# Spreading the 32x32 inversions of an RWKV-7 mixer over all 128 partitions of GpSimd

## The chip, the cores and the metric

The kernel runs on one core of one Trainium2 chip. The core has a matmul engine (TensorE, in the profile PE), a vector engine (DVE), a scalar engine (ACT), a general engine (GpSimd, in the profile POOL) and a queue that mostly issues transfers (SP). ACT and POOL issue transfers too. The metric is the device time of one execution in microseconds (us), from three runs.

## The reference, cut to what matters

The program computes two layers of a streaming encoder over 512 frames of width 1024. Layer 0 has two mixers side by side, HGRN2 (four heads of 128) and RWKV-7 (eight heads of 64), then a feed-forward block. Layer 1 has an S5 and an mLSTM mixer, then another feed-forward block. The change touches the RWKV-7 mixer alone. Its recurrence per head is

```python
def step(state, inp):
    r_t, w_t, k_t, v_t, a_t, b_t = inp
    sa = jnp.einsum("bhvk,bhk->bhv", state, a_t)
    state = (state * w_t[:, :, None, :] + sa[..., None] * b_t[:, :, None, :]
             + v_t[..., None] * k_t[:, :, None, :])
    return state, jnp.einsum("bhvk,bhk->bhv", state, r_t)
```

The kernel does this in chunks of 64 frames. Within a chunk the term with `sa` makes a triangular system: one strictly triangular 64x64 matrix per head and chunk, of which the inverse of one plus it (up to sign) is wanted. The kernel inverts the two 32x32 blocks on the diagonal of each and joins them by matmuls afterwards.

## The kernel before, in words

Activations lie as features x frames, so a matmul of the dense projections has 128 features of weights standing and 512 frames moving. Weights are f32; each is split into a rounded part `hi` (ACT, L375) and a rest `lo` (DVE or, for a few units, POOL, L376), and three matmuls into the PSUM tile `d` stand for one exact product. Those `d` matmuls are most of PE's work.

While PE does the dense projections of layer 0 (generator `dense`, called F), the mixers run beside it. `PRM["prog"]` lists seven stages; in each, `weave` takes turns between F up to a marker and one or two RWKV-7 generators, by the numbers that they yield. For RWKV-7 the eight heads make four pairs p, two pairs a group q, and the eight chunks make two halves g, so each kind of work comes four times, once for each (q, g):

- `rwp` (gates and `rw_prep`): elementwise work on DVE and ACT and small matmuls into PSUM tiles `r`. At its end four ACT-issued transfers per pair write the 32x32 blocks of `pb` to the scratch tensor `scr_a` in HBM.
- `inv` (`rw_inverse`): reads the 32 blocks of (q, g) into the tile `iu`, one block per partition, sets the diagonal to one, and sweeps: step j of 1 to 30 multiplies column j above the diagonal by row j to its right (`ti`, L987) and adds it to the rows above (L989). Both are POOL instructions. The result goes to `scr_u` in HBM (L991).
- `rwd` (`rw_solve` and `rw_chain`): eight transfers (L1000) bring the blocks of `scr_u` into the block-diagonal tile `ub`, then matmuls `r<-y,ub` and so on solve the system and carry the state from chunk to chunk.

The stages are: F alone; rwp(0,0); inv(0,0) with rwp(0,1); inv(0,1) with rwd(0,0); rwd(0,1) with rwp(1,0); inv(1,0) with rwp(1,1); inv(1,1) with rwd(1,0). F stands beside all but the last. After them rwd(1,1) runs beside the first part of layer 0's output projection (`outa`, matmuls `d<-ysp`).

The HGRN2 head in F has a chain of its own: for each of six levels an elementwise difference of `c` (`e<-c`, partly on POOL, partly on DVE), an exponential on ACT, two products on DVE (`e<-e,u` and `e<-e,k`) and matmuls `m<-e`.

The order in which the code emits instructions is not final. A scheduler of the framework places them by its own model of their durations, engine by engine, under the data dependencies; every engine then executes its list strictly in order. All tiles of the pool `pl` are allocated once, and `iu` and `ti` have one buffer each. Transfers of the inversions (`dq(1)`, `dq(2)`, `dq(3)`) are all issued by POOL, those into `scr_a` by ACT.

Of the kernel before, what the change touches and what calls it, by code (L numbers as in the profile page):

```python
# [10 lines left out]
F32 = mybir.dt.float32  # L11
# [4 lines left out]
ADD, SUB, MUL, MAX, MIN = ALU.add, ALU.subtract, ALU.mult, ALU.max, ALU.min  # L16

P = 128
# [184 lines left out]
def trunk(ctx: ExitStack, tc: tile.TileContext, A, out, dbg=None, start=0):  # L203
    nc = tc.nc
    V, S, G, T = nc.vector, nc.scalar, nc.gpsimd, nc.tensor
# [103 lines left out]
    if start < 1:  # L309
        for s in PRM["seq"]:  # L310
            nm, a, b = {"L": ("wB", 0, 1), "P": ("wB", 1, 3), "H": ("wA", 0, 4)}[s[0]]
# [54 lines left out]
    def wget(nm):  # L366
        assert order[pos[0]][0] == nm, (nm, order[pos[0]])
        while pos[1] <= pos[0] + AHEAD and pos[1] < len(order):
            wissue()
        pos[0] += 1  # L370
        return ready[pos[0] - 1]
# [283 lines left out]
    def layer0():  # L655
# [43 lines left out]
        scr_a = dram.tile([2, 2, 2, 2, 2, 4, 32, 32], F32, name="scr_a")  # L699
        scr_u = dram.tile([2, 2, 2, 2, 2, 4, 32, 32], F32, name="scr_u")  # L700
# [4 lines left out]
        N2 = 256  # L705
# [4 lines left out]
        pl = sl.pool("rw")  # L710
# [181 lines left out]
        def dq(j):  # L892
            return {"s": nc.sync, "g": G, "a": S}[PRM["dq"][j]]
# [84 lines left out]

        def rw_inverse(q, g):

            iu = pl.tile([32, 32, 32], F32, tag="iu", name="iu")
            dq(1).dma_start(iu, scr_a[q, g].rearrange("p h b c s t -> (p h b c) s t"))
            G.memset(iu.rearrange("p a b -> p (a b)")[:, 0:1024:33], 1.0)
            for j in range(1, 31):
                n = 31 - j
                t3 = pl.tile([32, N2], F32, tag="ti", name="ti")[:, 0:j * n].rearrange("p (a b) -> p a b", b=n)
                G.tensor_tensor(t3, iu[:, j:j + 1, j + 1:].to_broadcast([32, j, n]),  # L987
                                iu[:, 0:j, j:j + 1].to_broadcast([32, j, n]), MUL)
                G.tensor_tensor(iu[:, 0:j, j + 1:], iu[:, 0:j, j + 1:], t3, ADD)  # L989
                yield 1.2  # L990
            dq(2).dma_start(scr_u[q, g].rearrange("p h b c s t -> (p h b c) s t"), iu)  # L991

        def rw_solve(g, p):
            R = which[g, p]
# [136 lines left out]
        sa = Pools()  # L1131
        pa = sa.pool("hg", side="right")
        kinds = dict(rwp=rwp, rwd=rwd, inv=rw_inverse, gates=rw_gates, prep=rw_prep, solve=rw_solve, chain=rw_chain)

        def build(s):
# [87 lines left out]
    if start < 1:  # L1223
# [5 lines left out]
        for u in range(4):  # L1229
            w = wget("wO0b")  # L1230
            for i in range(2):
                n = 2 * u + i
# [445 lines left out]
    for u in range(4):  # L1678
        w = wget("wO1b")
        for i in range(2):  # L1680
            n = 2 * u + i
# [67 lines left out]
```

## Time and profile before

| what | value |
|---|---|
| time, median of 3 runs | 1464.06 us (1461.65 to 1466.17) |
| the profiled execution's own time | 1462.31 us |
| its span, first to last instruction | 1460.5 us |
| PE busy | 1400.2 us, 96% |
| DVE busy | 961.2 us, 66% |
| ACT busy | 681.1 us, 47% |
| POOL busy | 354.0 us, 24% |
| mean granted clock of PE | 0.976 |

The span is 1.8 us shorter than the profiled execution's time. A group row of the profile reads: line, engine, operation, out<-in by tile names, shapes, count, then busy us and mean ns of one, then the idle time of the engine just before such instructions and what ended it. A window row gives, for a stretch of the span, each engine's busy us, the clock that PE was granted (1.00 is full) and the share of the 16 DMA engines in use. The four inversions lie at about 91 to 134, 156 to 194, 273 to 314 and 333 to 375 us.

### The profile page before, as it was taken

To read this page: it belongs to the slowest core of one execution; us is meant where nothing else is said; L and a number is where in the kernel's file an instruction comes from. 1 tells how busy PE (TensorE), PEld (TensorE's weight loads), DVE (VectorE), ACT (ScalarE), POOL (GpSimd) and SP (SyncE) were. 2 spreads that over 40 slices of the span, in tenths; PEclk is the share of its full clock that TensorE was granted. 3 is DMA by queue.
4 is the path that set the end of the run, shared out by engine and by line. 5 is a ranking of instruction groups with operands and counts; after the bars stand their busy time and mean duration, and the time that the engine had idled before them with its cause. 6 is when DMAs were issued, how large, how long until landed. Compare 5 with 4: busy or idle time off the path is not lost.

```text
span 1460.5 us, 19910 instructions
## 1 busy us (share of the span) xinstructions
PE 1400.2 (96%) x6668; PEld 1136.9 (78%) x6668; DVE 961.2 (66%) x2041; ACT 681.1 (47%) x1594; POOL 354.0 (24%) x538
## 2 busy tenths in 40 slices
PE   8989999988999999999999899999999999999996
PEld 5877878766787788888888678766678888888885
DVE  7588679899688656555444688678776555554433
ACT  7554565636365333344333333477554434433332
POOL 5367650668420333110010542100020000000001
PEclk9988999999999999999999999999999999999998
DMA  5311221111323332333343842410133233333331
GB/s 180 94 38 46 64 72 52 30 46 58 118 84 97 101 116 91 113 108 106 105 125 105 206 113 80 116 58 28 56 105 90 99 101 96 92 102 94 93 114 61
DMA packets 51142, 133.39 MB, mean 91 GB/s; under 512 B 10640, under 2 KB 16272, under 8 KB 50784
## 3 DMA queue, kind: packets, MB, share of 16 engines
q1 hardware_dynamic: 38656, 116.86, 26.4%
q0 software_dynamic: 3024, 7.26, 2.1%
q10 hardware_dynamic: 9360, 8.00, 1.8%
q8 instruction: 53, 0.87, 0.2%
q14 instruction: 49, 0.40, 0.1%
HBM read 121.71 MB, written 10.39 MB: 90 GB/s over the span
## 4 chain that ended last, share of the span: by engine, by line
PE 76%; DVE 11%; POOL 4%; ACT 4%; DMA 2%; issue 2%; ACTq 0%; SPq 0%; DVEq 0%; POOLq 0%
PE d L292 63%; PE m L292 7%; PE r L292 5%; DVE lo L376 2%; POOL iu L989 1%; POOL ti L987 1%; DVE e L277 1%; DMA raw<-in_wV_dram 1%; ACT s L253 1%; DVE hl L467 1%; DVE ks L277 1%; ACT hi L375 0%; DVE u L277 0%; POOL ks L277 0%; DMA x<-in_xT_dram 0%
## 5 line engine op out<-in xcount | busy, mean ns | idle before, releaser
L375 ACT CAST hi<-raw 128x256 fp32r<-128x256 f32 (+1 forms) x809 | 317.4, 402 | 502.1 <-PE d L292 446.8
L376 DVE TENSOR_TENSOR lo<-raw,hi 128x256 fp32r<-128x256 f32 (+1 forms) x774 | 348.3, 460 | 280.5 <-ACT hi L375 269.6
L292 PE MATMUL d<-hh,hi 128*128 128x512 f32 x1088 | 436.1, 401 | 3.6 <-DVE ur L1086 2.4
L292 PE MATMUL d<-hh,lo 128*128 128x512 f32 x1088 | 431.4, 397 | 0.0
L292 PE MATMUL d<-hl,hi 128*128 128x512 f32 x1088 | 430.2, 395 | 0.0
L292 PEld LDWEIGHTS d<-hh,hi 128*128 128x128 f32 x1088 | 207.1, 190 | 48.0 <-DVE ur L1086 3.0
L292 PEld LDWEIGHTS d<-hh,lo 128*128 128x128 f32 x1088 | 206.8, 190 | 43.7 <-issue 1.5
L292 PEld LDWEIGHTS d<-hl,hi 128*128 128x128 f32 x1088 | 206.9, 190 | 43.3 <-issue 2.3
L292 PE MATMUL d<-ah,hi 128*128 128x512 f32 x330 | 128.4, 389 | 0.0
L292 PE MATMUL d<-al,hi 128*128 128x512 f32 x330 | 128.4, 389 | 0.0
L292 PE MATMUL d<-ah,lo 128*128 128x512 f32 x330 | 128.4, 389 | 0.0
L1718 POOL TENSOR_TENSOR x<-x,f 128x256 f32<-128x256 f32 x6 | 5.2, 889 | 358.8 <-issue 352.3
L292 PE MATMUL d<-ysp,hi 128*128 128x512 f32 x224 | 75.3, 411 | 2.7 <-DVE x L1685 1.5
L473 POOL TENSOR_TENSOR rstd<-rstd,sq 128x512 f32<-128x512 f32 x21 | 28.8, 1373 | 196.8 <-ACT sq L253 196.7
L989 POOL TENSOR_TENSOR iu<-iu,ti 32x30 f32<-32x30 f32 (+14 forms) x120 | 70.8, 590 | 9.2
L292 PEld LDWEIGHTS d<-ah,hi 128*128 128x128 f32 x330 | 61.9, 188 | 13.0
L292 PEld LDWEIGHTS d<-ah,lo 128*128 128x128 f32 x330 | 61.9, 188 | 12.8
L292 PEld LDWEIGHTS d<-al,hi 128*128 128x128 f32 x330 | 61.9, 188 | 12.8
L987 POOL TENSOR_TENSOR ti<-iu 32x30 f32<-32x30 f32 (+14 forms) x120 | 68.9, 574 | 9.0
L292 PEld LDWEIGHTS d<-ysp,hi 128*128 128x128 f32 x224 | 42.2, 193 | 12.9 <-DVE x L1685 2.3
L292 PE MATMUL d<-ysp,lo 128*128 128x512 f32 x112 | 45.5, 406 | 0.0
L1197 DVE TENSOR_TENSOR g<-d,g 128x512 f32<-128x512 f32 x42 | 29.0, 691 | 24.1 <-PE d L292 24.1
(490 smaller groups left out, 2043.0 us busy)
## 6 DMA issues: line engine op xcount, KB each, us to landing
raw<-in_wGU_dram SPq DMA_DIRECT2D x88, 512.0 KB, 3.6
raw<-in_wD_dram SPq DMA_DIRECT2D x32, 512.0 KB, 3.5
raw<-in_wA_dram SPq DMA_DIRECT2D x16, 512.0 KB, 3.7
raw<-in_wB_dram SPq DMA_DIRECT2D x13, 512.0 KB, 3.7
raw<-in_wD_dram SPq DMA_DIRECT2D x16, 384.0 KB, 3.1
raw<-in_wV_dram SPq DMA_DIRECT2D x6, 512.0 KB, 5.7
raw<-in_wQ_dram SPq DMA_DIRECT2D x6, 512.0 KB, 3.6
raw<-in_wK_dram SPq DMA_DIRECT2D x6, 512.0 KB, 3.7
```

Of the source, the lines that this page charges most:

```text
L253: a = S.activation(o, i, f, bias=bias, scale=scale)
L277: on(op, i, j).tensor_tensor(o, a, b, f)
L292: T.matmul(o, w, a, start=start, stop=stop)
L375: S.copy(h, src)
L376: eng.tensor_tensor(l, src, h.bitcast(F32), SUB)
L467: V.scalar_tensor_tensor(self.hl[:, k, :], x, pc(self.g, k), self.hh[:, k, :].bitcast(F32), MUL, SUB)
L473: self.eng.tensor_tensor(self.rstd, self.rstd, sq, ADD)
L987: G.tensor_tensor(t3, iu[:, j:j + 1, j + 1:].to_broadcast([32, j, n]), iu[:, 0:j, j:j + 1].to_broadcast([32, j, n]), MUL)
L989: G.tensor_tensor(iu[:, 0:j, j + 1:], iu[:, 0:j, j + 1:], t3, ADD)
L1197: V.tensor_tensor(g1, pu_, g1, MUL)
L1718: G.tensor_tensor(x[k][:, t], x[k][:, t], r_, MUL)
```

## The change

The 32 blocks of one (q, g) are laid on 128 partitions: partition 32k + n holds, of block n, the rows k, k+4, k+8 and so on, eight rows in the tile `iw`. Row j, which every partition needs at step j and which no earlier step alters, is read from a full copy of the block in `iu`, so each of the four groups of 32 partitions has its own copy. Step j then covers ceil(j/4) rows on every partition instead of j rows on a quarter of them; rows at or below j are zero in column j and stay as they are. The diagonal of ones is set at the end, in four pieces. The loads become eight transfers (four of 32 KB, four of 128 KB), the store four (32 KB each), all still issued by POOL. The generator yields 0.6 a step instead of 1.2.

```diff
         def rw_inverse(q, g):
-            iu = pl.tile([32, 32, 32], F32, tag="iu", name="iu")
-            dq(1).dma_start(iu, scr_a[q, g].rearrange("p h b c s t -> (p h b c) s t"))
-            G.memset(iu.rearrange("p a b -> p (a b)")[:, 0:1024:33], 1.0)
+            iu = pl.tile([P, 32, 32], F32, tag="iu", name="iu")
+            iw = pl.tile([P, 8, 32], F32, tag="iw", name="iw")
+            blocks = scr_a[q, g].rearrange("p h b c s t -> (p h b c) s t")
+            for k in range(4):
+                w = slice(32 * k, 32 * k + 32)
+                dq(1).dma_start(iw[w], blocks.rearrange("n (r k) t -> n k r t", k=4)[:, k])
+                dq(1).dma_start(iu[w], blocks)
             for j in range(1, 31):
-                n = 31 - j
-                t3 = pl.tile([32, N2], F32, tag="ti", name="ti")[:, 0:j * n].rearrange("p (a b) -> p a b", b=n)
-                G.tensor_tensor(t3, iu[:, j:j + 1, j + 1:].to_broadcast([32, j, n]),
-                                iu[:, 0:j, j:j + 1].to_broadcast([32, j, n]), MUL)
-                G.tensor_tensor(iu[:, 0:j, j + 1:], iu[:, 0:j, j + 1:], t3, ADD)
-                yield 1.2
-            dq(2).dma_start(scr_u[q, g].rearrange("p h b c s t -> (p h b c) s t"), iu)
+                n, m = 31 - j, (j + 3) // 4
+                t3 = pl.tile([P, 80], F32, tag="ti", name="ti")[:, 0:m * n].rearrange("p (a b) -> p a b", b=n)
+                G.tensor_tensor(t3, iu[:, j:j + 1, j + 1:].to_broadcast([P, m, n]),
+                                iw[:, 0:m, j:j + 1].to_broadcast([P, m, n]), MUL)
+                G.tensor_tensor(iw[:, 0:m, j + 1:], iw[:, 0:m, j + 1:], t3, ADD)
+                yield 0.6
+            for k in range(4):
+                w = slice(32 * k, 32 * k + 32)
+                G.memset(iw[w].rearrange("p a b -> p (a b)")[:, k:256:36], 1.0)
+                dq(2).dma_start(scr_u[q, g].rearrange("p h b c s t -> (p h b c) s t")
+                                .rearrange("n (r k) t -> n k r t", k=4)[:, k], iw[w])
```

What the scheduler makes of it differs in three places that matter below. The first is POOL's list at the start of the first inversion, before the change (`e` and `c` are tiles of the HGRN2 head, `lo`, `raw` and `hi` the split of a weight):

```order
L982 DMA iu<-scr_a 32x1024
L376 TENSOR_TENSOR lo<-raw,hi 128x256
L983 MEMSET iu 32x32
L987 TENSOR_TENSOR ti<-iu 32x30
L989 TENSOR_TENSOR iu<-iu,ti 32x30
L987 TENSOR_TENSOR ti<-iu 32x58
L277 TENSOR_TENSOR e<-c 128x8x32
L277 TENSOR_TENSOR e<-c 128x16x16
L989 TENSOR_TENSOR iu<-iu,ti 32x2x29
```

The same place after the change; three of the four pairs of loads and three of the five `e<-c` stand just above these rows:

```order
L277 TENSOR_TENSOR e<-c 128x64x4
L277 TENSOR_TENSOR e<-c 128x128x2
L987 DMA iw<-scr_a 32x8x32
L988 DMA iu<-scr_a 32x1024
L376 TENSOR_TENSOR lo<-raw,hi 128x256
L999 MEMSET iw 32x8
L992 TENSOR_TENSOR ti<-iu,iw 128x30
L994 TENSOR_TENSOR iw<-iw,ti 128x30
L992 TENSOR_TENSOR ti<-iu,iw 128x29
```

All five `e<-c`, which stood between steps of the inversion, now stand ahead of its first step, between the loads. The second place is the fourth inversion on POOL, before the change, after its seventh step:

```order
L987 TENSOR_TENSOR ti<-iu 32x168
L989 TENSOR_TENSOR iu<-iu,ti 32x7x24
L277 TENSOR_TENSOR e<-c 128x64x4
L277 TENSOR_TENSOR e<-c 128x128x2
L987 TENSOR_TENSOR ti<-iu 32x184
```

And after the change, ahead of its first step:

```order
L987 DMA iw<-scr_a 32x8x32
L277 TENSOR_TENSOR e<-c 128x64x4
L277 TENSOR_TENSOR e<-c 128x128x2
L988 DMA iu<-scr_a 32x1024
L987 DMA iw<-scr_a 32x8x32
L988 DMA iu<-scr_a 32x1024
L999 MEMSET iw 32x8
L992 TENSOR_TENSOR ti<-iu,iw 128x30
```

The last two `e<-c` of the fourth HGRN2 head no longer stand behind fourteen instructions of the inversion. The third place is PE's list in the stage of the first inversion, before the change (`m<-e` are the HGRN2 levels, `r` matmuls belong to RWKV-7, `d` to the projections):

```order
L292 MATMUL d<-hh,hi 128x512
L292 MATMUL m<-e_1026,e_1025 128x128 x4
L292 MATMUL m<-e 128x64 x4
L971 MATMUL r<-con,bb_225 128x128 x4
L292 MATMUL r<-ek,ak_233 128x64 x4
L971 MATMUL r<-con,kb_231 128x128 x4
L292 MATMUL d<-hl,hi 128x512
```

And after it:

```order
L971 MATMUL r<-con,bb_225 128x128 x2
L292 MATMUL m<-e_1026,e_1025 128x128 x4
L971 MATMUL r<-con,bb_225 128x128 x2
L292 MATMUL r<-ek,ak_233 128x64 x4
L971 MATMUL r<-con,kb_231 128x128 x4
L971 MATMUL r<-con,bb_227 128x128 x3
L292 MATMUL m<-e 128x64 x4
```

Some `d` matmuls move a few places here. Of PE's 5948 listed matmuls and transposes, 62 change their place relative to the others, all between the 346th and the 649th; before and behind that, PE's list is the same. No list of DVE, ACT or SP gains or loses an instruction; POOL's gains 52.

## The prediction

> **What bounds the kernel now.** I read the page first, then PE's waits where the mixers of layer 0 run, then windows over the inversions, then the groups of DVE instructions inside and outside them.
>
> ```profile
> PE 1400.2 (96%) x6668; PEld 1136.9 (78%) x6668; DVE 961.2 (66%) x2041; ACT 681.1 (47%) x1594; POOL 354.0 (24%) x538
> ...
> PE m L292 <- DVE e L277: 5.4, 7, 2.4
> PE r L959 <- ACT y L281: 5.1, 1, 5.1
> PE r L292 <- DVE c L932: 3.0, 2, 2.4
> PE m L292 <- DVE st L810: 2.8, 2, 2.2
> ...
> PE r L292 <- DMA ub<-scr_u: 1.2, 1, 1.2
> ```
>
> PE is busy 96% of the span, so no change to POOL can win more than PE's 60 us of idle time and what its lowered clock costs. The waits (60 to 430 us; total us, times, longest) say who holds PE up there: mostly DVE. Only one wait, of 1.2 us, is for the inversions' result, `ub`. So how long an inversion takes is not in itself on the path. What it does to DVE may be.
>
> ```profile
> 91.00:112.00 21.00, 18.50 (x96) 15.14 (x95) 19.38 (x30) 14.36 (x35) 19.12 (x33) 0.80 0.06 24
> 112.00:134.00 22.00, 22.00 (x103) 17.70 (x102) 17.11 (x38) 12.37 (x34) 19.19 (x34) 0.80 0.08 25
> 156.00:194.00 38.00, 37.76 (x219) 31.55 (x218) 24.94 (x53) 21.15 (x59) 32.79 (x62) 1.00 0.18 57
> 272.00:284.00 12.00, 11.39 (x73) 9.38 (x74) 11.72 (x28) 8.24 (x22) 10.51 (x23) 1.00 0.07 23
> 284.00:292.00 8.00, 8.00 (x29) 6.34 (x29) 6.19 (x11) 4.40 (x13) 7.21 (x11) 0.57 0.00 1
> 292.00:300.00 8.00, 5.75 (x37) 4.39 (x36) 7.96 (x15) 5.40 (x13) 7.21 (x11) 0.88 0.15 43
> 300.00:315.00 15.00, 15.00 (x66) 12.44 (x65) 13.19 (x28) 6.74 (x17) 13.09 (x22) 0.84 0.08 22
> 333.00:356.00 23.00, 19.77 (x151) 17.60 (x150) 22.55 (x43) 13.67 (x31) 20.65 (x36) 0.94 0.16 47
> ```
>
> Columns: length, then busy us of PE, PE's weight loads, DVE, ACT, POOL, then clock and DMA share. DVE is full (92 to 99%) and PE is not in 91 to 112, 272 to 284, 292 to 300 and 333 to 356: there DVE sets the pace. In 112 to 134, 156 to 194, 284 to 292 and 300 to 315 PE is full or nearly so, at 0.57 to 0.84 of its clock in all but the second.
>
> ```profile
> L376 DVE TENSOR_TENSOR lo<-raw,hi 128x256 fp32r<-128x256 f32 x4 | 1.5, 418 | 0.0
> L277 DVE TENSOR_TENSOR e<-e,u 128x256 f32<-128x256 f32 x6 | 4.6, 786 | 0.0
> L277 DVE TENSOR_TENSOR e<-e,k 128x256 f32<-128x256 f32 x6 | 4.2, 707 | 0.0
> L277 DVE TENSOR_TENSOR e<-c 128x256 f32<-128x256 f32 x5 | 4.0, 811 | 0.0
> ...
> L376 DVE TENSOR_TENSOR lo<-raw,hi 128x256 fp32r<-128x256 f32 x6 | 4.4, 769 | 0.0
> L277 DVE TENSOR_TENSOR e<-e,k 128x256 f32<-128x256 f32 x4 | 3.0, 745 | 0.0
> L277 DVE TENSOR_TENSOR ar<-raw,er 128x256 f32<-128x256 f32 x2 | 1.6, 849 | 0.0
> ...
> L376 DVE TENSOR_TENSOR lo<-raw,hi 128x256 fp32r<-128x256 f32 x2 | 2.3, 1172 | 0.0
> L277 DVE TENSOR_TENSOR e<-e,k 128x256 f32<-128x256 f32 x5 | 3.2, 637 | 0.0
> L277 DVE TENSOR_TENSOR e<-c 128x256 f32<-128x256 f32 x4 | 2.1, 552 | 0.0
> ...
> L810 DVE SCALAR_TENSOR_TENSOR st<-st,ec,m 128x128 f32<-128x128 f32 x6 | 2.1, 345 | 0.1
> L810 DVE SCALAR_TENSOR_TENSOR st<-st,ec,m 128x128 f32<-128x128 f32 x6 | 2.1, 345 | 0.2
> ```
>
> The first row is 314 to 329 us, where no inversion runs: 418 ns for two SBUF inputs of 128x256. The three blocks behind it are 91 to 112, 272 to 300 and 333 to 356, where one does: the same shape takes 552 to 1172 ns. The last two rows are an operation with one input in PSUM (`m`), at 196 to 258 us and in the fourth inversion: 345 and 345. So DVE operations with both inputs in SBUF are held up by POOL's inversion, the others are not.
>
> **The change part by part.**
>
> *The sweep.* Sixty instructions an inversion before and after, but each with fewer elements per partition: the sum over the steps of j(31-j) is 4960, of ceil(j/4)(31-j) 1424, so the mean falls from 165 to 47.
>
> ```profile
> 156.37 0.23 POOL L987 TENSOR_TENSOR ti<-iu 32x30 f32<-32x30 f32 x1
> 156.67 0.23 POOL L989 TENSOR_TENSOR iu<-iu,ti 32x30 f32<-32x30 f32 x1
> ...
> 172.96 0.60 POOL L987 TENSOR_TENSOR ti<-iu 32x240 f32<-32x240 f32 x1
> ...
> L989 POOL TENSOR_TENSOR iu<-iu,ti 32x30 f32<-32x30 f32 (+14 forms) x120 | 70.8, 590 | 9.2
> L987 POOL TENSOR_TENSOR ti<-iu 32x30 f32<-32x30 f32 (+14 forms) x120 | 68.9, 574 | 9.0
> L277 POOL TENSOR_TENSOR e<-c 128x256 f32<-128x256 f32 x30 | 21.0, 720 | 54.0 <-PE r L1049 44.7 <-PE m L731 4.5 <-DVE u L277 3.4
> ```
>
> Where DVE leaves it alone, one takes 0.23 us for 30 elements and 0.60 for 240, so 1.76 ns an element, and starts follow 0.07 us behind the end. At 47 elements that is 0.26 + 0.07 = 0.33 us, 20 us an inversion; now it is 0.58 + 0.07, 39 us, and with the `e<-c` between, up to 42. Does an instruction on 128 partitions cost what it costs on 32? The nearest row says nearly: `e<-c` at 128x256 takes 720 ns on average. If all of the 720 against 600 were due to partitions, the sweep would be 23 us; I take 20 to 23.
>
> *What DVE gets back.* Above 418 ns the groups quoted lose, in 91 to 112, 6 x 0.37 + 6 x 0.29 + 5 x 0.39 = 5.9 us; in 272 to 300, 6 x 0.35 + 4 x 0.33 + 2 x 0.43 = 4.3; in 333 to 356, 2 x 0.75 + 5 x 0.22 + 4 x 0.13 = 3.1. Together 13.3, without smaller groups. In the first stretch some of it is due to POOL's own five `e<-c` (5 x 0.72 of POOL's 19.12 us, a fifth), which stay: 12.1 is the inversions'. Two ways to scale it. If DVE simply shares with POOL, its loss goes with the time that the sweep runs, 20/40: half stays and 6 us comes back. If a DVE operation waits for the POOL instruction in progress to end, the loss also goes with that instruction's length, 0.26/0.58: 0.22 stays and 9.4 comes back. The 1172 ns of `lo` fit the second better: 0.75 us more is about one whole POOL instruction. I take 9. Below, 0 if what DVE gains is not on the path; above, 13, since groups left out lose too.
>
> [...]
>
> *The wait for `ub`* (1.2 us) goes if the fourth inversion ends at least that much earlier relative to PE. Its parts:
>
> ```profile
> L982 POOL DMA_DIRECT2D iu<-scr_a x4 | 2.2, 560 | 23.6 <-DMA scr_a<-pb 15.6 <-DVE e L281 7.7 <-PE d L292 0.4
> ...
> L1404 POOL DMA_DIRECT2D ub<-scr_c x8: 564/793/903, 832.0 to 837.7; - x8
> ...
> iu<-scr_a POOLq DMA_DIRECT2D x4, 128.0 KB, 2.8
> ub<-scr_u POOLq DMA_DIRECT2D x32, 16.0 KB, 2.2
> ...
> ub<-scr_c POOLq DMA_DIRECT2D x8, 64.0 KB, 7.3
> scr_y<-yg POOLq DMA_DIRECT2D x8, 64.0 KB, 4.4
> ```
>
> Ten more issues at 0.56 us (0.90 at most, as in L1404) are 5.6 to 9 us of POOL. The loads land in 2.8 us as now, or in 7.3 as the eight loads from `scr_c` do, issued back to back in equally small pieces; the stores in 2.2 to 4.4. Against 17 to 22 us less sweep, the inversion ends 2 to 14 us earlier. DVE's gain makes PE ask up to 9 us earlier, so the wait may stay: 1.2 counts half, 0.6. For the other three inversions PE never waits for `ub`, so their added transfers are covered by the shorter sweep.
>
> *Behind the new issues* stand POOL's `e<-c` and one `lo`. In the first inversion four issues (2.2 us) come ahead of the first `e<-c` instead of one, but no step of the sweep stands between the five any more; in the fourth the last two lose fourteen instructions ahead of them. I count 0. *PE's moved matmuls* are the same work in another order: 0, with the clock as rival below.
>
> **Sum:** -9 - 0.6, about -10 us of 1462.31, the profiled execution's time: 1452. The three runs shown have a median 1.75 higher, so I forecast 1454.
>
> **The rivals.**
>
> *No change: PE takes back what DVE frees.* For it: PE's busy time does not fall, and the clock is low just where DVE frees it.
>
> ```profile
> 104.00:108.00 4.00, 3.86 (x20) 2.77 (x19) 3.74 (x7) 3.65 (x10) 3.61 (x6) 0.87 0.00 0
> 108.00:112.00 4.00, 4.00 (x14) 2.76 (x13) 3.20 (x6) 1.23 (x4) 3.61 (x6) 0.50 0.00 0
> 112.00:116.00 4.00, 4.00 (x14) 3.04 (x13) 2.02 (x4) 1.07 (x3) 3.61 (x6) 0.50 0.02 4
> 116.00:120.00 4.00, 4.00 (x20) 2.95 (x20) 2.60 (x6) 2.54 (x9) 3.61 (x6) 0.50 0.00 0
> ```
>
> After the gap at 94 to 97 PE ran 12 us at half clock, worth 6 us, and the list is reordered just there. If such a stretch is added, 6 of the 10 us go; with another in the third inversion (0.57 and 0.88 now), all: 1462. Against it: fewer gaps should give fewer such stretches. [...]
>
> *Much faster.* The clock recovers with the gaps: 0.20 of 43 us in 91 to 134 and 0.43, 0.12 and 0.16 of 8, 8 and 15 us in 284 to 315 are 15 us; half of that on top gives 1447.
>
> *Slower: the added transfers delay weights.* Each inversion reads 640 KB instead of 128, and stores in small pieces. A weight tile is
>
> ```profile
> raw<-in_wGU_dram SPq DMA_DIRECT2D x88, 512.0 KB, 3.6
> ```
>
> so 512 KB more are 3.6 us of the DMA engines, and with small pieces at most twice that. If PE waited through 5 us of it four times, 20 us are lost and 10 won: 1474. It decides once a weight tile lands after PE wants it. Against it: the DMA share is 0.06 to 0.18 in the window rows above, and no PE wait for a weight is among those quoted.
>
> *The change does not do what it says* (POOL instructions no shorter): time 1464 or a little more; the rows by size speak against it.
>
> **How the numbers follow.** Forecast 0.50 (own range 1449 to 1459), much faster 0.16, no change 0.21 with the last rival, slower 0.13. A difference under 0.3% (4.4 us) can't be told from none here. Faster holds the forecast, the second, and little of the third: 0.66; same 0.21; slower 0.13. The range reaches into the rivals on both sides: 1444 to 1467.
>
> **What would show it.** In the profile after, POOL's sweeps about 20 us long with instructions near 0.3 us; `lo` at 128x256 near 450 to 550 ns in the inversions; DVE still full but shorter in the stretches named; PE's total idle time some 6 to 10 us less. Wrong if the DVE rows don't fall, or fall without PE's waits falling, or if the mean clock drops below 0.976 by 0.005 (7 us), or if PE waits for `hi` or `lo`.

## The result and the profile after

The changed kernel takes 1449.32 us (median of 4 runs, 1446.87 to 1452.43) against 1463.87 before: a ratio of 0.990, with a 95% interval of 0.9882 to 0.9919, so 12 to 17 us less. The profiled execution took 1446.87 us. The forecast was 1454 us in a range of 1444 to 1467, and faster.

First from the page, the cores view and PE's waits between 60 and 430 us of the kernel after (total us, times, longest):

```profile
PE 1391.6 (96%) x6668; PEld 1131.5 (78%) x6668; DVE 935.9 (65%) x2041; ACT 680.1 (47%) x1594; POOL 320.6 (22%) x590
...
core 0: 1445.1 us, clock 0.980
...
PE r L959 <- ACT y L281: 4.6, 1, 4.6
PE m L292 <- DVE e L277: 4.5, 7, 2.0
PE r L292 <- DVE c L932: 2.4, 1, 2.4
PE d L292 <- DVE x L1183: 1.9, 1, 1.9
```

DVE executes the same 2041 instructions in 25.3 us less. PE's waits for DVE's `st` (2.8 us) and `ur` (2.3) are gone from the list, and so is the wait for `ub` (1.2). Of the 15.4 us by which the span is shorter, 6.8 are PE's idle time (span less PE busy: 60.3 us before, 53.5 after); the other 8.6 are PE's busy time for the same 6668 instructions. Then the sweep, over all four inversions (ns, shortest, median, longest), and DVE's groups in the four (98 to 125, 158 to 182, 275 to 302, 331 to 357 us):

```profile
L992 POOL TENSOR_TENSOR ti<-iu,iw x120: 206/296/834, 100.1 to 356.6; 128x60 f32<-128x60 f32 x16, 128x28 f32<-128x28 f32 x8, 128x48 f32<-128x48 f32 x8, 128x42 f32<-128x42 f32 x8
L994 POOL TENSOR_TENSOR iw<-iw,ti x120: 209/303/823, 100.4 to 356.9; 128x60 f32<-128x60 f32 x16, 128x28 f32<-128x28 f32 x8, 128x48 f32<-128x48 f32 x8, 128x42 f32<-128x42 f32 x8
...
L376 DVE TENSOR_TENSOR lo<-raw,hi 128x256 fp32r<-128x256 f32 x6 | 2.7, 470 | 1.3 <-ACT hi L375 1.3
L277 DVE TENSOR_TENSOR e<-e,u 128x256 f32<-128x256 f32 x5 | 2.2, 438 | 1.7 <-ACT e L253 1.7
...
L376 DVE TENSOR_TENSOR lo<-raw,hi 128x256 fp32r<-128x256 f32 x9 | 4.1, 453 | 3.1 <-ACT hi L375 3.0
...
L376 DVE TENSOR_TENSOR lo<-raw,hi 128x256 fp32r<-128x256 f32 x8 | 3.5, 466 | 0.6 <-ACT hi L375 0.6
...
L376 DVE TENSOR_TENSOR lo<-raw,hi 128x256 fp32r<-128x256 f32 x3 | 1.4, 477 | 0.0
```

POOL's instructions have a median of 0.30 us, the sweeps last 25, 23, 27 and 26 us, and `lo` takes 453 to 477 ns beside them where it took up to 1172. One thing did not get better, in the first inversion (windows: length, busy us of PE, PEld, DVE, ACT, POOL, then clock and DMA share):

```profile
86.00:104.00 18.00, 15.44 (x96) 12.81 (x93) 12.54 (x26) 14.70 (x36) 12.70 (x27) 0.90 0.27 69
104.00:117.00 13.00, 13.00 (x46) 10.97 (x46) 7.29 (x15) 5.84 (x18) 10.65 (x31) 0.50 0.01 1
117.00:135.00 18.00, 18.00 (x102) 14.57 (x102) 15.40 (x41) 11.37 (x28) 13.25 (x35) 0.99 0.27 73
```

PE is full from 104 to 117 us at half its clock, with DVE idle for almost half of that time. What DVE gave back there did not all reach the end.

### The profile page after: what moved, and what is told of

It is laid out like the page before. It is cut to its first block, busy times and chain, and to the rows that moved or that the text cites. A ratio compares the mean times of both kernels' runs of the same rounds, so it can differ in the third digit from the quotient of the medians.

```text
span 1445.1 us, 19973 instructions
## 1 busy us (share of the span) xinstructions
PE 1391.6 (96%) x6668; PEld 1131.5 (78%) x6668; DVE 935.9 (65%) x2041; ACT 680.1 (47%) x1594; POOL 320.6 (22%) x590
## 4 chain that ended last, share of the span: by engine, by line
PE 81%; DVE 10%; ACT 3%; DMA 2%; issue 1%; POOL 1%; ACTq 0%; DVEq 0%; SPq 0%; POOLq 0%
PE d L292 67%; PE m L292 8%; PE r L292 5%; DVE lo L376 1%; DVE e L277 1%; DMA raw<-in_wV_dram 1%; DVE hl L467 1%; ACT s L253 1%; DVE ks L277 1%; DMA x<-in_xT_dram 1%; ACT hi L375 1%; DMA raw<-in_wA_dram 0%; DVE u L277 0%; POOL ks L277 0%; ACTq L952 0%
## 5 line engine op out<-in xcount | busy, mean ns | idle before, releaser
L376 DVE TENSOR_TENSOR lo<-raw,hi 128x256 fp32r<-128x256 f32 (+1 forms) x774 | 341.4, 452 | 284.1 <-ACT hi L375 279.7
L292 PEld LDWEIGHTS d<-al,hi 128*128 128x128 f32 x330 | 61.9, 188 | 12.8
L992 POOL TENSOR_TENSOR ti<-iu,iw 128x60 f32<-128x60 f32 (+10 forms) x120 | 41.0, 342 | 21.0 <-DMA iu<-scr_a 9.3
L1204 DVE TENSOR_TENSOR g<-d,rstd 128x512 f32<-128x512 f32 x42 | 29.0, 690 | 21.7 <-PE d L292 21.7
```

Of the source, the lines that this page charges most:

```text
L292: T.matmul(o, w, a, start=start, stop=stop)
L376: eng.tensor_tensor(l, src, h.bitcast(F32), SUB)
L992: G.tensor_tensor(t3, iu[:, j:j + 1, j + 1:].to_broadcast([P, m, n]), iw[:, 0:m, j:j + 1].to_broadcast([P, m, n]), MUL)
L1204: V.tensor_tensor(g1, pg, rstd, MUL)
```

## The experiments

All but the change were timed in five rounds, and the ratio is to the kernel before on the same chip. Runs of different rounds are compared by the ratio, because the kernel before itself had medians from 1461.6 to 1464.2 us there. Us are 1464 times the ratio's distance from one.

| run | median us | ratio (95%) | us against before |
|---|---|---|---|
| the change | 1449.3 | 0.990 (0.9882 to 0.9919) | -14.6 |
| memset_sweep | 1442.2 | 0.9861 (0.9834 to 0.9889) | -20.3 |
| nosweep_b | 1442.1 | 0.9873 (0.9848 to 0.9898) | -18.6 |
| nosweep_a | 1448.7 | 0.9891 (0.987 to 0.9911) | -16.0 |
| long128 | 1473.7 | 1.006 (1.0039 to 1.0081) | +8.8 |
| mul3 | 1510.0 | 1.0299 (1.0274 to 1.0325) | +43.8 |
| sp_mul2 | 1454.1 | 0.994 (0.9921 to 0.996) | -8.8 |
| sp_load | 1443.9 | 0.9861 (0.9839 to 0.9884) | -20.3 |
| few_dma | 1472.7 | 1.0079 (1.0062 to 1.0096) | +11.6 |
| long_few | 1484.9 | 1.0157 (1.0137 to 1.0178) | +23.0 |
| few_mul2 | 1505.2 | 1.0298 (1.0279 to 1.0318) | +43.6 |
| one_load | 1441.5 | 0.9845 (0.9821 to 0.9869) | -22.7 |
| late_loads | 1440.1 | 0.9851 (0.9828 to 0.9874) | -21.8 |

### Is it POOL's reading that holds DVE up?

**memset_sweep**, the kernel before with

```diff
-                t3 = ...
-                G.tensor_tensor(t3, iu[:, j:j + 1, j + 1:].to_broadcast([32, j, n]), ..., MUL)
-                G.tensor_tensor(iu[:, 0:j, j + 1:], iu[:, 0:j, j + 1:], t3, ADD)
+                G.memset(iu[:, 0:18], 0.0)
+                G.memset(iu[:, 0:18], 0.0)
```

> The kernel before with each of the 60 sweep instructions of an inversion replaced by a memset of 32x576 (so the inverse is not computed; loads, stores, number of instructions and PE's order are those of before): POOL is as busy for as long, but reads nothing. Theory A (it is POOL's reading of SBUF against DVE's two inputs that holds DVE up): DVE's lo and e near 0.42 us in the inversions, 1448 to 1453 if the gain needs no new order. Rival D (any POOL instruction holds DVE up, or POOL's time itself sets the end): lo at 0.5 to 0.75, 1460 to 1465. Rival B (order): about 1463, with DVE's operations faster all the same.

`lo` in the first inversion of the kernel before (91 to 134 us); then, of memset_sweep, the memsets over all inversions, `lo` in the first (90 to 132 us), and the span with its clock:

```profile
L376 DVE TENSOR_TENSOR lo<-raw,hi 128x256 fp32r<-128x256 f32 x7 | 3.7, 527 | 0.4 <-ACT hi L375 0.3
...
L987 POOL MEMSET iu<- x120: 567/568/864, 92.7 to 353.5; 32x576 f32 x120
...
L376 DVE TENSOR_TENSOR lo<-raw,hi 128x256 fp32r<-128x256 f32 x8 | 3.4, 421 | 0.5 <-ACT hi L375 0.3 <-ACT c L253 0.2
...
core 0: 1439.4 us, clock 0.987
```

POOL is busy with 0.57 us instructions for as long as before, PE's order is nearly that of before (20 of its 6668 instructions moved), and `lo` takes 421 ns instead of 527: its whole loss is gone, and the kernel is 16 to 24 us faster, more than the 1448 to 1453 us that theory A had. So neither POOL's time, nor an earlier end of the inversion, nor PE's new order is needed for the gain.

**nosweep_b** and **nosweep_a**, the kernel before and the change with the two instructions of a step removed, so that no inverse is computed, and all transfers kept:

```diff
             for j in range(1, 31):
                 ...
-                G.tensor_tensor(..., MUL)
-                G.tensor_tensor(..., ADD)
                 yield ...
```

> The change with the sweep left out (the inverse is not computed; all loads, memsets and stores stay, PE in the order of the change): what is left to win from POOL's instructions. Theory A with a loss by length: DVE's lo in the change still takes 0.40 to 0.47 us against 0.42 elsewhere, so 0 to 3 us are left: 1446 to 1449. Rival A2 (loss by POOL's busy time): as much again as the change brought, for half the sweep is still there: 1437 to 1443.

> The kernel before with the sweep left out (the inverse is not computed): one load of 128 KB and one store an inversion as before, but PE in the order of the change. It splits the 6.5 us between the run without sweep (1448.7) and the run with memsets (1442.2), which differ in the loads and stores and in PE's order. If the sixteen more issues and transfers of the change cost that: 1440 to 1443. If PE's order (two short waits in place of one, and the half clock behind the one of 2.0 us) costs it: 1447 to 1450.

(The change has ten more issues an inversion, not sixteen.) The change is within 2 us of the same kernel without any sweep: of the sweep's price almost nothing is left. Both runs without sweep have the change's PE order. The one with the transfers of before is 6.6 us faster by the medians, but they are of different rounds: by the ratios it is 2.6 us, and the two intervals overlap. So these two alone do not show a price of the loads; they are taken up below.

### The length of an instruction, or the time that POOL is busy?

**long128**, the change with the element counts of before on each partition:

```diff
-                n, m = 31 - j, (j + 3) // 4
+                n, m = 31 - j, j
                 ...
-                                iw[:, 0:m, j:j + 1].to_broadcast([P, m, n]), MUL)
-                G.tensor_tensor(iw[:, 0:m, j + 1:], iw[:, 0:m, j + 1:], t3, ADD)
+                                iu[:, 0:m, j:j + 1].to_broadcast([P, m, n]), MUL)
+                G.tensor_tensor(iu[:, 0:m, j + 1:], iu[:, 0:m, j + 1:], t3, ADD)
                 ...
```

The memsets and the stores take `iu` in the same way, and the loads into `iw` are half as large.

> The change with its instruction length undone: every step covers all j rows on all 128 partitions (each of the four groups of 32 sweeps its whole copy; the loads into iw stay, of half their rows, and are not used), so POOL has the 128 partitions, the loads, the stores and, but for a few neighbours, the order of the change, with the element counts of before. Theory A (DVE operations with two SBUF inputs are held up in proportion to the length of POOL's instructions): POOL instructions of 0.58 to 0.65 us, DVE's lo in the inversions back at 0.55 to 0.75 us, 1458 to 1466. Rival B (the gain is from the new order, above all the e<-c that no longer stand between the steps): about 1450. Rival C (a POOL instruction on 128 partitions costs more than on 32): instructions over 0.7 us and more than 1466.

The additions over all inversions of the kernel before and of long128, then `lo` in the first (99 to 141 us) and a wait of PE in long128:

```profile
L989 POOL TENSOR_TENSOR iu<-iu,ti x120: 226/598/1080, 91.2 to 374.8; 32x30 f32<-32x30 f32 x8, 32x58 f32<-32x58 f32 x8, 32x84 f32<-32x84 f32 x8, 32x108 f32<-32x108 f32 x8
...
L994 POOL TENSOR_TENSOR iu<-iu,ti x120: 238/607/1594, 99.7 to 384.2; 128x30 f32<-128x30 f32 x8, 128x58 f32<-128x58 f32 x8, 128x84 f32<-128x84 f32 x8, 128x108 f32<-128x108 f32 x8
...
L376 DVE TENSOR_TENSOR lo<-raw,hi 128x256 fp32r<-128x256 f32 x8 | 5.3, 677 | 0.1
...
PE r L292 <- DMA ub<-scr_u: 6.9, 2, 4.7
```

With long instructions the loss is back (677 ns, even more than the 527 before) and the gain gone, on 128 partitions as on 32. Four times the partitions cost little: a median of 607 ns against 598. The time is above theory A's 1458 to 1466; the change's loads and stores come on top of the long sweep, and PE waits 6.9 us for `ub` instead of 1.2.

**mul3**, the change with each product three times:

```diff
                 G.tensor_tensor(t3, ..., MUL)
+                G.tensor_tensor(t3, ..., MUL)
+                G.tensor_tensor(t3, ..., MUL)
                 G.tensor_tensor(iw[:, 0:m, j + 1:], iw[:, 0:m, j + 1:], t3, ADD)
```

> The change with each product of the sweep computed three times into the same tile: 120 POOL instructions an inversion instead of 60, each as short as in the change, PE in the order of the change, and a sweep as long as before, near 40 us. Theory A1 (a DVE operation waits for the POOL instruction in progress: what it loses goes with that instruction's length): DVE's lo at 0.45 to 0.50 us as in the change, and most of the gain stays: 1450 to 1455. Rival A2 (DVE shares with POOL, so its loss goes with the time that POOL is busy): lo in the inversions at 0.55 to 0.70 us, 1458 to 1464. The later end of the fourth inversion could cost a wait for ub of some us on either.

`lo` in the first inversion (100 to 151 us), and PE's waits between 60 and 460 us:

```profile
L376 DVE TENSOR_TENSOR lo<-raw,hi 128x256 fp32r<-128x256 f32 x15 | 6.5, 461 | 1.1 <-ACT hi L375 1.1
...
PE r L292 <- DMA ub<-scr_u: 37.0, 3, 18.4
PE m L292 <- DVE e L277: 22.1, 4, 19.1
```

Both theories missed the time. `lo` at 461 ns bears out A1: twice the instructions cost each DVE operation no more (453 to 477 ns in the change). But the sweeps now last 48 to 53 us, and with the longer loads that is past the slack: PE stands 37 us before `ub`. The run says how dear an inversion becomes once it is late; its time says nothing clean on A1 against A2. So:

**sp_load** and **sp_mul2**, loads issued by SP, and the same with each product twice:

```diff
-PRM = {..., 'dq': 'aggg', ...}
+PRM = {..., 'dq': 'asgg', ...}
```

> The change with its eight loads an inversion issued by SP instead of POOL; stores stay on POOL. PE is back in the order of before but for two matmuls; on POOL the five e<-c of a HGRN2 head stand together ahead of the sweep, with no issue between them. If the 6.6 us that the two runs without sweep lay apart were POOL's issues ahead of e<-c (the price of the loads): 1441 to 1445, faster than the change. If it was the transfers themselves, or if SP's weights come later behind eight issues that wait for scr_a: 1448 to 1460.

> The run with loads by SP, with each product computed twice: 90 short instructions, a sweep near 30 us, still shorter than before, and no e<-c between its steps, so that the later end of the inversion stays inside its slack as far as that can be had; PE and DVE in the order of the run with loads by SP. If DVE's loss goes with the length of POOL's instructions: within 3 us of that run. If it goes with the time that POOL is busy: 5 to 8 us slower. If waits for ub show up, the slack of the inversion is under 10 us.

`lo` in the first inversion of sp_load (97 to 123 us) and of sp_mul2 (97 to 137 us):

```profile
L376 DVE TENSOR_TENSOR lo<-raw,hi 128x256 fp32r<-128x256 f32 x7 | 3.0, 430 | 0.5 <-ACT hi L375 0.3 <-ACT c L253 0.2
...
L376 DVE TENSOR_TENSOR lo<-raw,hi 128x256 fp32r<-128x256 f32 x8 | 3.5, 439 | 0.5 <-ACT hi L375 0.3 <-ACT c L253 0.2
```

sp_load lies inside the 1441 to 1445 us of its first theory; its interval just touches that of the change. In sp_mul2 the first sweep lasts 40 us instead of 26 (the expectation had 30). Yet `lo` takes 439 ns instead of 430, and DVE is busy for 936.3 us of the whole span instead of 936.2: the loss does not go with POOL's time. Still sp_mul2 is 10 us slower, which is outside both theories. PE's waits after 315 us and two rows of POOL's timeline in sp_mul2 say where:

```profile
PE m L292 <- DVE e L277: 7.0, 1, 7.0
PE r L959 <- ACT y L281: 5.3, 1, 5.3
PE r L292 <- DMA ub<-scr_u: 3.0, 1, 3.0
...
322.97 4.36 POOL L1012 DMA_DIRECT2D ub<-scr_u  x8 [2.28 <-DMA scr_u<-iw]
327.39 1.85 POOL L277 TENSOR_TENSOR e<-c 128x256 f32<-128x256 f32 x3
```

In sp_load PE waits 1.0 us for `e` after 315 us, and none for `ub`. The third inversion ends too late; behind its store stand the eight issues for `ub` (4.36 us), and behind those the `e<-c` of the last HGRN2 head. These two waits, 9 us more than in sp_load, are nearly all of the difference. So an inversion has two deadlines: `ub`, and the `e<-c` that queue behind it on POOL.

### What the loads cost

**few_dma**, the change with one transfer for each of iw, iu and the store:

```diff
-            for k in range(4):
-                w = slice(32 * k, 32 * k + 32)
-                dq(1).dma_start(iw[w], blocks.rearrange("n (r k) t -> n k r t", k=4)[:, k])
-                dq(1).dma_start(iu[w], blocks)
+            dq(1).dma_start(iw, bass.AP(blocks.tensor, blocks.offset, [[32, 4], [1024, 32], [128, 8], [1, 32]]))
+            dq(1).dma_start(iu, bass.AP(blocks.tensor, blocks.offset, [[0, 4], [1024, 32], [32, 32], [1, 32]]))
```

and the store likewise. **long_few** is long128 with one such load of `iu`, **few_mul2** is few_dma with each product twice.

> The change with two loads and one store an inversion instead of eight and four (the four groups of partitions in one descriptor list each, the copies of iu by a source that repeats): same bytes into the same places, the same sweep. PE, DVE, ACT then have exactly the order of before. If DVE's relief is the whole gain and needs no new order: as the memset run or a little above, 1441 to 1446, faster than the change. If the order of the change is part of its gain: 1450 to 1458.

> The sweep of before with its element counts, but on 128 partitions (each group of 32 sweeps its whole copy), loaded by one transfer; PE and DVE in the order of before. If partitions cost nothing and long128 lost its 9.5 us by its order and by later loads: 1461 to 1467, with DVE's lo near 0.7 us in the inversions. If 128 partitions cost more than 32 of themselves: 1470 to 1476.

> The run with few transfers, with each product of the sweep computed twice: 90 short instructions an inversion, a sweep near 30 us, shorter than before, so that no later end of an inversion hides the answer as it did with three products; PE and DVE in the order of before. If DVE's loss goes with the length of POOL's instructions: within 3 us of the run with few transfers. If it goes with the time POOL is busy: 5 to 8 us slower than it (half of what the change gained).

All three were slower than before, and slower than any of their theories had. The transfers of few_dma (KB, us to landing), then of the change; POOL's timeline in few_dma; and its window while `iu` lands:

```profile
iu<-scr_a POOLq DMA_DIRECT2D x4, 512.0 KB, 12.8
iw<-scr_a POOLq DMA_DIRECT2D x4, 128.0 KB, 7.5
scr_u<-iw POOLq DMA_DIRECT2D x4, 128.0 KB, 9.7
...
iu<-scr_a POOLq DMA_DIRECT2D x16, 128.0 KB, 2.6
iw<-scr_a POOLq DMA_DIRECT2D x16, 32.0 KB, 2.5
scr_u<-iw POOLq DMA_DIRECT2D x16, 32.0 KB, 1.9
...
102.75 0.24 POOL L990 TENSOR_TENSOR ti<-iu,iw 128x30 f32<-128x30 f32 x1 [7.34 <-DMA iu<-scr_a]
...
104.20 0.67 POOL L277 TENSOR_TENSOR e<-c 128x256 f32<-128x256 f32 x1
...
96.70:100.10 3.40, 3.40 (x19) 3.40 (x18) 3.29 (x9) 2.88 (x7) 0.00 (x0) 0.50 0.25 94
```

A list with all of `iu` lands 12.8 us after its issue, one with a quarter of it 2.6 us after its own, and while the long list lands the share of the DMA engines in use is 0.25 (96.70 to 100.10 us); why no more, no run here shows. From the first issue of an inversion to the first step of its sweep it is 13.4 to 17.0 us in few_dma and 10.2 to 12.4 in the change. POOL's third `e<-c` stands behind a sweep that waits 7.34 us for `iu`. So the other two runs say nothing clean on length or partitions either. What they share with mul3 is the lesson that transfer time comes off the slack.

**one_load**, the change with `iw` copied out of `iu`:

```diff
-                dq(1).dma_start(iw[w], blocks.rearrange("n (r k) t -> n k r t", k=4)[:, k])
                 dq(1).dma_start(iu[w], blocks)
+            for k in range(4):
+                w = slice(32 * k, 32 * k + 32)
+                G.tensor_copy(iw[w], iu[w].rearrange("p (r k) t -> p k r t", k=4)[:, k])
```

> The change with iw copied out of iu by four POOL copies of 32x256 instead of four loads (four issues an inversion less); PE in the order of the change but for three matmuls. If each issue ahead of e<-c costs its share of the 6.6 us: about half back, 1445 to 1448. If it hangs on whether the short wait of PE behind e<-c falls below what keeps the clock up: all of it or nothing, 1441 to 1443 or 1449. Copies hold DVE up as other POOL reads do, some 0.1 us each: nothing that can be seen.

**late_loads**, one_load with the four loads of `iw` back, behind those of `iu`:

```diff
             for k in range(4):
                 w = slice(32 * k, 32 * k + 32)
                 dq(1).dma_start(iu[w], blocks)
+            for k in range(4):
+                dq(1).dma_start(iw[w, 0:8], blocks.rearrange("n (r k) t -> n k r t", k=4)[:, k, 0:8])
             for k in range(4):
                 w = slice(32 * k, 32 * k + 32)
                 G.tensor_copy(iw[w], iu[w].rearrange("p (r k) t -> p k r t", k=4)[:, k])
```

> The run with copies, with the change's four loads of iw put back at full size, but behind the loads of iu, so that in the first inversion they stand behind the five e<-c instead of between them (the copies write the same values again); PE and DVE in exactly the order of the run with copies, eight loads as in the change. If what the change still paid for its loads was their place ahead of e<-c (PE waits 2.0 us there, and the clock is halved behind it): 1440 to 1444, PE's wait for e in the first inversion near 1 us. If it was their number or their transfers: 1447 to 1450.

In the new loop of late_loads `w` keeps its last value. So all four loads go to partitions 96 to 127 of `iw`, one after another (POOL waits 3.5, 1.8 and 1.8 us for them in the first inversion), and the copies then overwrite them: the result is right, but only the last copy writes the values that a load had put there. The number of loads and their bytes are those of the change, their target is not, and the first sweep begins at 108.4 us instead of 100.1.

Both runs beat the change, one_load by all of the price and not by half; their intervals and its do not overlap. With the eight loads and their bytes back, and a first sweep that begins 8 us later, late_loads is as fast as one_load: what the change paid was neither the number of its loads nor their bytes, but their place ahead of `e<-c`. DVE and POOL in the first inversion, of the change and then of late_loads:

```profile
95.10 0.50 POOL L988 DMA_DIRECT2D iu<-scr_a  x1
95.61 1.30 POOL L277 TENSOR_TENSOR e<-c 128x256 f32<-128x256 f32 x2
...
95.40 2.38 DVE L277 TENSOR_TENSOR e<-c 128x256 f32<-128x256 f32 x1
...
94.44 1.48 POOL L277 TENSOR_TENSOR e<-c 128x256 f32<-128x256 f32 x2 [0.31 <-PE m L292]
...
94.49 0.95 DVE L277 TENSOR_TENSOR e<-c 128x256 f32<-128x256 f32 x1
```

In the change the issues move POOL's last two `e<-c` so that DVE's own `e<-c`, begun 0.21 us before them, lasts through both and beyond: 2.38 us, against 0.95 in late_loads, where it begins just after the first of them. PE waits 2.0 us for it instead of 1.1. The copies themselves hold DVE up by little: `e<-e,k` beside them takes 0.45 us in one_load (at 97.14 us) and 0.47 in late_loads (96.72), against 0.41 in the change (98.63). In the traces of the kernel before and of the change every stretch of half clock, but for the one at the end of the span, lasts 3.41, 6.83, 13.65 or 17.07 us, a multiple of 3.41. The next rows are such windows of 3.41 us around PE's wait, of the change and then of late_loads:

```profile
97.04:100.46 3.42, 1.41 (x14) 1.36 (x13) 3.23 (x8) 1.01 (x4) 2.03 (x6) 1.00 0.38 75
100.46:103.87 3.41, 3.41 (x16) 2.64 (x16) 1.38 (x4) 2.76 (x7) 2.71 (x10) 0.50 0.33 129
...
95.17:98.58 3.41, 2.35 (x22) 2.12 (x21) 3.41 (x7) 1.93 (x6) 3.21 (x6) 1.00 0.10 28
98.58:102.00 3.42, 3.42 (x26) 2.89 (x26) 2.90 (x8) 3.31 (x8) 0.84 (x3) 1.00 0.54 161
```

In the change PE is busy for 1.41 us of a window and the next one has half the clock, which lasts to the end of the window 104 to 117 us shown above (100.46 to 117.5 us, five windows); in late_loads PE is busy for 2.35 and the clock stays full. Half of 17 us is 8.5, and late_loads and the change are 7 apart. The other runs fit: over 86 to 136 us the mean clock is 0.83 before, in the change and in nosweep_a, and 1.00 in late_loads, one_load, memset_sweep and nosweep_b. nosweep_a and nosweep_b have the same order on PE, so it is the loads that set these two apart there. Only sp_load (0.90) and sp_mul2 (0.86) lie between. Over all timed executions the mean clock is 0.9775 in the change and 0.985 in late_loads.

## Why the prediction was right or wrong

The sign, the range and the mechanism on DVE's side were right; the time was 4.7 us too high (1454 against 1449.3), from two errors that partly cancel: the clock that recovers was left out, and so was the price of the new issues. That the time came so near is in part luck.

- *The sweep* was put at 20 to 23 us and lasts 23 to 27. The estimate took undisturbed instructions, and POOL's own are held up too: in the first inversion one of 128x60 takes 0.29 us with DVE idle (at 112.32 us) and 0.56 beside a DVE scan (116.73); the median of all is 0.30, the longest 0.83. Partitions cost about nothing, as assumed (long128: a median of 607 ns on 128 against 598 on 32).
- *What DVE gets back.* Scaling by instruction length was right. Above 418 ns `lo` kept 35 to 59 ns in the inversions, of 109 to 754 before. Over all of `lo` at 128x256 from 60 to 400 us the mean is 510 ns before, 433 in the change and 419 in nosweep_a: 0.15 of the loss stays, and the sum, which let 0.78 of 12.1 us come back, took 0.22. Not all that it counted was the inversions': at 196 to 258 us before, where none runs, `e<-e,u` takes 645 ns, beside POOL's own `e<-c`. Simple sharing of time, the other way to scale it, falls with mul3 and sp_mul2 on `lo` (461 and 439 ns), and the memset run (421) shows that it is POOL's reading.
- *The term was mis-sized all the same.* It took 9 us, with 13 as its end, all of it from PE's waits. The reading of the sweep of before cost 20 us (memset_sweep). DVE's time fell by more than the sum had (25.3 us, not 9 to 13), but most of that was not on the path: PE's idle time fell by 6.8 us in the change and by 6.1 in memset_sweep. The rest, 8.6 and 15.0 us, is PE's busy time, and that is mostly the clock: the profile of memset_sweep shows a mean of 0.987 instead of 0.976, and 0.011 of 1439 us is 16 us. Over all timed executions it is 0.984 in memset_sweep, and 0.9745 for the kernel before in the same rounds. The forecast had this as the rival "much faster" and left it out of the sum.
- *The wait for `ub`* was counted half and went altogether.
- *Behind the new issues: "I count 0"* is the step that failed. They cost about 7 us (the change against late_loads), not by the 2.2 us that they take, but by when DVE and POOL then meet, and by the clock behind that. That is the rival "PE takes back what DVE frees", in the one place that it named: by the windows (length times one less the clock, twice) PE had 17 us of half clock in the first inversion before (91 to 134 us) and 17 us after (86 to 135). The rival's own reading needs a correction: behind the gap at 94 to 97 us the half clock lasted for one window; the 12 us at half clock that it named stand behind a window from 103.54 to 106.95 us in which PE was busy for 3.27 us.
- *The added transfers* delayed no weight. In the change PE waits for no transfer, and for the two parts of a weight as long as before (`hi` 6.9 us against 6.4, `lo` 0.7 against 0.6). POOL's transfers went from 2.1 to 2.8% of the DMA engines' span, about 2.5 us an inversion, against the 3.6 that the rival took from a whole weight tile; its "at most twice that" for small pieces was the author's estimate. The rival's price of 20 us had the wrong queue: few_dma shows that late loads cost as much as that through POOL's own queue.

In round numbers: 20 us were to be had from POOL's reads, 1 to 2 of them are still in the short sweep, some 4 to 7 went for the place of the loads, and 14.6 are left. Each of these is uncertain by 2 to 4 us.

Open: what else halves the clock in that place. In sp_load PE waits nowhere near it for more than 0.5 us, and yet (windows of 3.41 us, columns as above)

```profile
101.35:104.77 3.42, 3.42 (x20) 2.56 (x20) 2.88 (x7) 3.37 (x9) 2.87 (x8) 1.00 0.00 0
104.77:108.20 3.43, 3.43 (x12) 2.18 (x11) 1.73 (x4) 1.96 (x6) 2.88 (x8) 0.50 0.00 0
```

a full window is followed by a half one. The kernel before has nearly the same at 103.54 us (PE busy 3.27 us), and the change has it at 277.94 us, where a full window (3.42 us) is followed by two of half clock. So PE's busy time in the window before does not by itself tell whether the clock halves; what else does, no run settles. The split between PE's waits and the clock, in the change and in memset_sweep, is also from single profiles; over the timed executions of the kernel before in the five rounds the mean clock lies between 0.969 and 0.980.

## What to carry to other kernels

Beside a busy VectorE, shorten the single GpSimd instruction that reads SBUF, or let GpSimd only write: in the first inversion `lo` took 527 ns beside reading instructions of 0.6 us, 470 beside those of 0.3, and 421 beside memsets of 0.57. GpSimd's total time hardly mattered to DVE (439 ns with a sweep of 40 us, 430 with one of 26). Then ask what the new form does to GpSimd's queue: issues put ahead of small operations on which another chain waits cost about 7 us here, half of the gain, and copying out of data that has landed, or issuing later, cost nothing that shows (0.9845 and 0.9851 of the time before, 0.9873 with no sweep and the transfers of before). A side task has a slack on each thing that queues behind it, not only on its result: here sweeps of 40 us instead of 26 cost nothing until the third of them ended, and 9 us from there.

## What was not expected of the hardware

- A GpSimd memset of 0.57 us left `lo`, a DVE operation with two SBUF inputs, alone (421 ns, against 418 where no inversion runs); products and additions of about the same length (medians 0.58 and 0.60 us) did not (means of 527 to 1172).
- In the change a DVE operation that began 0.21 us ahead of two GpSimd ones without a gap between them was held through both (2.38 us, from 95.40; the same operation took 0.41 at 94.64).
- In few_dma 512 KB in one list landed in 12.8 us, with 0.25 of the DMA engines in use (96.70 to 100.10 us); of the change's four lists of 128 KB each landed in 2.6.
- In the change PE's clock was halved behind a 3.41 us window in which PE was busy for 1.41 us, with a single wait of 2.0 us. The busy time alone does not decide, though: full windows were followed by half clock too (above), in the kernel before one with 1.87 us (294.69 to 298.10) was, and in the run without sweep on the transfers of before one with 1.64 us kept the clock:

```profile
91.76:95.17 3.41, 1.64 (x8) 0.97 (x7) 3.41 (x5) 3.31 (x10) 2.54 (x5) 1.00 0.21 52
95.17:98.58 3.41, 3.34 (x31) 3.34 (x31) 3.35 (x10) 1.93 (x6) 2.10 (x3) 1.00 0.00 0
```
